# Warm-up matmuls, the row loads of the first norm, and the place of the second norm's scale in a one-core trunk layer

## The chip, the core and the metric

The kernel runs on one core of one Trainium2 chip. The metric is the device time of one execution in microseconds; the median of three runs is given. One further execution was recorded by the hardware profiler, and all lines of the profile and the trace below come from that one. The engines are named as the profile names them: PE (matrix multiply) and PEld (its weight loads), DVE (vector), ACT (scalar), POOL, and SP, which here only issues DMAs.

## What is computed

One layer of a trunk: 512 tokens of width 1024, one batch, all float32. Three residual steps follow each other: a mixer with four branches, a cross-attention to 256 memory tokens, and a convolutional feed-forward part. Cut to what matters here:

```python
def rms_norm(x, g):
    xf = x.astype(jnp.float32)
    y = xf * lax.rsqrt(jnp.mean(xf * xf, axis=-1, keepdims=True) + EPS)
    return (y * g.astype(jnp.float32)).astype(x.dtype)

def cross_attention(h, mem_n, wq, wkv, wo):
    ...
    q = (h @ wq).reshape(bsz, s, XA_HEADS, XA_HEAD_DIM)
    k, v = jnp.split(mem_n @ wkv, 2, axis=-1)
    ...
    sc = jnp.einsum('bshd,bmhd->bhsm', q, k).astype(jnp.float32) * (XA_HEAD_DIM ** -0.5)
    p = jax.nn.softmax(sc, axis=-1).astype(v.dtype)
    ...

    h = rms_norm(x, g[0])                       # first norm
    y = hybrid_mixer(h, w_in[l], ...)
    x = x + rms_norm(y, g[1])
    h = rms_norm(x, g[2])                       # second norm
    mem_n = rms_norm(mem, g[4])
    y = cross_attention(h, mem_n, xa_wq[l], xa_wkv[l], xa_wo[l])
    x = x + rms_norm(y, g[3])
    h = rms_norm(x, g[5])
    y = conv_ffn(h, ...)
    x = x + rms_norm(y, g[6])
```

## The kernel before

**Layout and arithmetic.** The activation is kept transposed: eight tiles x[k] of 128 features by 512 tokens. Every large product is done in three matmuls on two-part operands (`mm3`, L124): each operand is split into a rounded part (name ending in h or hi) that ACT writes by a cast, and a remainder (l or lo) that DVE writes by a subtraction; then hi·hi, hi·lo and lo·hi are added up in PSUM. Weights come in units of 512 KB: SP issues the load (L74), ACT casts (L75), DVE subtracts (L76), and PE uses the unit. The tiles raw, whi and wlo have four buffers each, so the cast of one unit waits until PE has done with the unit four before it.

**The first loop** (L242 to L271) runs over k = 0 to 7. For each k it loads x[k] (256 KB) and the rows of the v, a_lr and sgu-v weights (264 KB; for k = 0 in two pieces of 136 and 128 KB). ACT writes xgh, which is x[k] times the first norm's gain (L253), and casts the weights (L259, L267); DVE writes the remainders; PE then does 12 matmuls of 272 columns into four banks (va, L239) and 6 of 256 columns into two banks (sv, L239). The gains come by a small DMA of 32 bytes a partition on ACT's queue (gn0, L232). The per-token factor of the first norm is not in xg: it is applied later, as a per-partition scale, when the banks are read.

**The factor of the first norm** comes from a second copy of x, laid out in rows of tokens: `RowNorm` (L198) loads eight tiles of 128 tokens by 512 features (row, L207, 256 KB each, 2 MB in all) and ACT squares each with a running sum (L208). `step(n)` does n of them; `rstd()` does all that are still to do, and then the square root on ACT and the reciprocal on DVE (L194, L195). In the loop the eight steps are spread over k = 2 to 7 (L271). After the loop, `bcast_tok` (L216) spreads the factor over the partitions by matmuls with the identity (bctok), and rb0s keeps a copy.

**Order of work.** The program is written in one stream, and a scheduler places the instructions on each engine's queue by its own estimate of when they can run. What is written inside `with tc.high_priority():` goes ahead of all other work that its inputs allow it to pass. That covers `rs0 = xnorm.rstd()` and `rb0 = bcast_tok(rs0)` at L272 to L274. On the chip every engine then takes its queue in order, and DMAs issued by SP go through one queue.

**The second norm** (`residual1`, L701 to L727) runs on DVE and ACT while PE computes keys and values of the memory (L730 to L750). It adds the mixer's output to x, sums the squares into s2, turns s2 into a factor per token by four small matmuls (`rstd_tok`, L181, sumtok), spreads that by four more (bctok), and then writes h2 = x·gain·factor in eight DVE instructions (L725), each followed by a cast and a subtraction (`split`, L150). `wq` (L756) multiplies h2 by the query weights; `scores` (L766) multiplies q by k, takes the maximum over the memory tokens (L779, L780) and the exponential with the scale 1/16 (L783).

Of the kernel before, what the change touches and what calls it, by code (L numbers as in the profile page):

```python
# [16 lines left out]
P = 128  # L17
# [6 lines left out]
EPS = 1e-6  # L24

NSLOT = 76
LOOK = 2
POOL_OUT = (0, 2, 3, 5)

# [10 lines left out]
def tile_trunk(ctx: ExitStack, tc: tile.TileContext, a: dict, out: bass.AP):  # L40
# [13 lines left out]
    def get(name, dt=F32):  # L54
        i = free.pop(0)
        serial[0] += 1
        t = sp.tile([P, S], dt, tag=f"s{i}", name=f"{name}_{serial[0]}")
        held[id(t)] = (i, t)
        return t
# [105 lines left out]
    def gcol(n, k):  # L165
        return pc("norm", n * KT + k)

    ident = cp.tile([P, P], F32, name="ident")
    make_identity(nc, ident)
    ones = cp.tile([P, 1], F32, name="ones")  # L170
# [57 lines left out]
    VA = 256 + 16  # L228
    vps = [bank("B", f"va{t}") for t in range(4)]
    sps = [bank("A", f"sv{t}") for t in range(2)]  # L230
    gn0 = cp.tile([P, KT], F32, name="gn0")
    scalar.dma_start(gn0, a["par"][:, 0:KT])  # L232
    xg, svw = [], []
    xnorm = RowNorm(a["x_rows"], 4, "rs0")

# [4 lines left out]
                              start=k == 0 and i == 0, stop=k == KT - 1 and i == 2)  # L240

    for k in range(KT):  # L242
        sync.dma_start(x[k], a["xT"][k])
        raw = wp.tile([P, 1024], F32, tag="raw", bufs=4, name=f"rawv{k}")
        if k == 0:
            sync.dma_start(raw[:, 0:VA], a["w_vs"][k][:, 0:VA])
            sync.dma_start(raw[:, VA:VA + 256], a["w_vs"][k][:, VA:VA + 256])
        else:
            sync.dma_start(raw[:, 0:VA + 256], a["w_vs"][k])
        if k == 4:  # L250
            sync.dma_start(par, a["par"])
        hi, lo = get("xgh", F32R), get("xgl", F32R)
        scalar.activation(hi, x[k], AF.Copy, scale=gn0[:, k:k + 1])  # L253
        wh = wp.tile([P, 1024], F32R, tag="whi", bufs=4, name=f"whv{k}")
        wl = wp.tile([P, 1024], F32R, tag="wlo", bufs=4, name=f"wlv{k}")
        if k == 0:
            vector.tensor_copy(wh[:, 0:VA], raw[:, 0:VA])
        else:
            scalar.copy(wh[:, 0:VA], raw[:, 0:VA])  # L259
        vector.scalar_tensor_tensor(lo, x[k], gn0[:, k:k + 1], hi.bitcast(F32), op0=ALU.mult, op1=ALU.subtract)  # L260
        vector.tensor_tensor(wl[:, 0:VA], raw[:, 0:VA], wh[:, 0:VA].bitcast(F32), op=ALU.subtract)
        xg.append((hi, lo))
        if k % 2 == 0:
            svw.append((get("svwh", F32R), get("svwl", F32R)))
        c = slice((k % 2) * 256, (k % 2 + 1) * 256)
        sh, sl = svw[-1][0][:, c], svw[-1][1][:, c]
        scalar.copy(sh, raw[:, VA:VA + 256])  # L267
        vector.tensor_tensor(sl, raw[:, VA:VA + 256], sh.bitcast(F32), op=ALU.subtract)
        rows(vps, k, (wh[:, 0:VA], wl[:, 0:VA]), range(4))
        rows(sps, k, (sh, sl), (0, 1))  # L270
        xnorm.step((0, 0, 1, 1, 1, 1, 2, 2)[k])  # L271
    with tc.high_priority():  # L272
        rs0 = xnorm.rstd()
        rb0 = bcast_tok(rs0)  # L274
# [426 lines left out]
    def residual1():  # L701
        with tc.high_priority():
            rs = rstd_tok([ssum[0]], "rs1")
            rb = bcast_tok(rs)
        put(ssum[0])
        s2 = []
        for k in range(KT):
            vector.tensor_tensor(yg[k], rb, yg[k], op=ALU.mult)
            vector.tensor_add(x[k], x[k], yg[k])
            put(yg[k])  # L710
            sq = get("sq")
            scalar.activation(sq, x[k], AF.Square)
            if k == 0:
                s2.append(sq)
            else:
                vector.tensor_add(s2[0], s2[0], sq)
                put(sq)
        with tc.high_priority():
            rs = rstd_tok(s2, "rs2")
            rb = bcast_tok(rs)  # L720
        put(*s2)
        h2 = []
        for k in range(KT):
            hk = get("h2")
            vector.scalar_tensor_tensor(hk, x[k], gcol(2, k), rb, op0=ALU.mult, op1=ALU.mult)  # L725
            h2.append(split(hk, "h2", True))
        return h2  # L727


    kk = [(get("kh", F32R), get("kl", F32R)) for _ in range(4)]  # L730
# [8 lines left out]
    for cb in range(2):  # L739
# [8 lines left out]
                        k == 0, k == KT - 1)  # L748
        for t in range(2):
            vv[t][cb] = split(ps[t], "v")  # L750
    h2 = residual1()
    for t in mem:
        put(*t)

# [11 lines left out]
    def scores(hd, q):  # L766
        pr = [get("p"), get("p")]
        for t2 in range(2):
            ps = bank("C", "sc")
            for i in range(2):  # L770
                t = 2 * t2 + i
                tt = slice(t * P, (t + 1) * P)
                for d in range(2):
                    c = slice(d * 256, (d + 1) * 256)
                    mm3(ps[:, i * 256:(i + 1) * 256], (q[d][0][:, tt], q[d][1][:, tt]),
                        (kk[hd][0][:, c], kk[hd][1][:, c]), d == 0, d == 1)
            serial[0] += 1
            mx = tp.tile([P, 4], F32, tag="mx", bufs=4, name=f"mx_{serial[0]}")
            vector.reduce_max(mx[:, 0:2], ps.rearrange("p (t m) -> p t m", t=2), axis=AX.X)  # L779
            vector.tensor_scalar(mx[:, 0:2], mx[:, 0:2], -1.0 / 16.0, None, op0=ALU.mult)  # L780
            for i in range(2):
                c = slice(i * 256, (i + 1) * 256)
                scalar.activation(pr[t2][:, c], ps[:, c], AF.Exp, bias=mx[:, i:i + 1], scale=1.0 / 16.0,  # L783
                                  accum_out=mx[:, 2 + i:3 + i])
            vector.reciprocal(mx[:, 2:4], mx[:, 2:4])
            for i in range(2):
                c = slice(i * 256, (i + 1) * 256)
                vector.tensor_scalar(pr[t2][:, c], pr[t2][:, c], mx[:, 2 + i:3 + i], None, op0=ALU.mult)
        for d in range(2):
            put(*q[d])  # L790
        return pr
# [198 lines left out]
def _layout(inp):  # L990
    import numpy as np
    i = {k: np.asarray(v) for k, v in inp.items()}

    def mt(w, width=P):
        k, m = w.shape
        return np.ascontiguousarray(
            w.reshape(k // P, P, m // width, width).transpose(2, 1, 0, 3).reshape(m // width, P, (k // P) * width))

    def cols(v):
        v = v.reshape(-1, v.shape[-1])  # L1000
        return v.reshape(v.shape[0], -1, P).transpose(2, 0, 1).reshape(P, -1)

    d = {}
    d["xT"] = np.ascontiguousarray(i["x"][0].T).reshape(KT, P, S)
    d["memT"] = np.ascontiguousarray(
        i["mem"][0].T.reshape(4, 2, P, NMEM).transpose(0, 2, 1, 3)).reshape(4, P, 2 * NMEM)
    w = i["w_in"][0]
    names = ("ab", "ac", "ax", "q", "k", "v", "r", "alr", "su", "sv", "rx", "rg")
    widths = (256,) * 7 + (16,) + (256,) * 4
    seg, o = {}, 0  # L1010
    for n, wd in zip(names, widths):
        seg[n] = w[:, o:o + wd]
        o += wd
    d["w_in"] = mt(np.concatenate([seg[n] for n in ("k", "q", "rx", "su", "rg", "ac", "ax", "ab", "r")], axis=1))
    d["x_rows"] = i["x"][0].reshape(4, P, D)
    d["mem_rows"] = i["mem"][0].reshape(2, P, D)

    def moving(w):
        k, m = w.shape
        return np.ascontiguousarray(  # L1020
            w.reshape(k // 256, 2, P, m // S, S).transpose(3, 0, 2, 1, 4).reshape(-1, P, 2 * S))

    d["w_vs"] = np.concatenate([seg["v"], seg["alr"], seg["sv"]], axis=1).reshape(KT, P, 528)
    d["par"] = np.ascontiguousarray(np.concatenate([
        cols(i["norm_g"][0]), cols(i["sc_conv_w"][0]), cols(i["gla_b_alpha"]), cols(i["gla_norm_g"]),
        cols(i["lru_conv_w"][0]), cols(i["lru_conv_b"]), cols(i["lru_b_a"]), cols(i["lru_b_x"]),
        cols(i["b_gate"][0]), cols(i["ffn_conv_w"][0]), cols(i["ffn_conv_b"])], axis=1))
    d["lam"] = np.ascontiguousarray(cols(i["lru_lambda"]))
    d["ln_g"] = i["sgu_ln_g"][0]
    d["ln_b"] = i["sgu_ln_b"][0]  # L1030
    d["sgu_wT"] = np.ascontiguousarray(i["sgu_w"][0].transpose(2, 0, 1)).reshape(P, S)
    d["sgu_b"] = i["sgu_b"][0]
    d["lru_w_a"] = i["lru_w_a"][0]
    d["lru_w_x"] = i["lru_w_x"][0]
    d["w_alpha"] = i["gla_w_alpha"][0]
    d["w_gate"] = mt(i["w_gate"][0])
    d["w_br"] = np.ascontiguousarray(
        i["w_branch"][0].reshape(4, 2, P, 2, 4, P).transpose(0, 3, 2, 4, 1, 5)).reshape(8, P, 1024)
    d["w_mix"] = mt(i["w_mix_out"][0])
    d["w_q"] = mt(i["xa_wq"][0])  # L1040
    d["w_k"] = mt(i["xa_wkv"][0][:, :D])
    d["w_v"] = moving(i["xa_wkv"][0][:, D:])
    d["w_o"] = mt(i["xa_wo"][0])
    d["w_up"] = mt(i["ffn_w_up"][0])
    d["w_down"] = mt(i["ffn_w_down"][0])
    return {k: np.ascontiguousarray(v) for k, v in d.items()}
# [20 lines left out]
```

## Time and profile before

| | us |
|---|---|
| median of three runs (lowest, highest) | 960.14 (959.26, 961.12) |
| time of the profiled execution | 960.77 |
| its span, from the first to the last instruction | 958.2 |
| busy PE | 943.9 |
| busy PEld | 800.5 |
| busy DVE | 575.0 |
| busy ACT | 420.7 |
| moved by DMA | 98.27 MB |

The span leaves out 2.57 us of the profiled execution's time. PE is busy for all but 14.3 us of the span; the rows that show where it waits are quoted in the prediction. The mean granted clock of PE is 0.997.

### The profile page before, as it was taken

The page shows a single profiled execution, that of the slowest core. Times are in us where ns is not written, and L with a number is a line of the kernel's source. Part 1 is how long each engine was busy: PE and PEld are TensorE (multiplying, and loading weights), DVE is VectorE, ACT ScalarE, POOL GpSimd, SP SyncE. Part 2 cuts the span into 40 slices and gives each one's busy share as a digit, 9 for nine tenths or more (in the row PEclk, how much of TensorE's full clock was granted, in tenths as well). Part 3 has the DMA queues.
Part 4 walks back from the last instruction along what each step waited for, and adds up shares of the span by engine and source line. Part 5 has one row for each costly group of instructions (what it writes and reads, how often), then busy time and mean ns, then how long its engine had stood idle before and what let it go on. Part 6 is the DMA issues. An engine that isn't in the chain of part 4 may idle for free.

```text
span 958.2 us, 12139 instructions
## 1 busy us (share of the span) xinstructions
PE 943.9 (99%) x4782; PEld 800.5 (84%) x4782; DVE 575.0 (60%) x886; ACT 420.7 (44%) x637; POOL 11.9 (1%) x33
## 2 busy tenths in 40 slices
PE   7999999999999999999999999999999999999996
PEld 7888888888888888898888899888888888888885
DVE  5877557445454667359854736887677776622404
ACT  7845336332323534455543645554444444332311
POOL 2000000000000000000000000000000000000001
PEclk9999999999999999999999999999999999999998
DMA  9432231322243422335412420232322323233302
GB/s 334 136 123 89 67 102 52 109 89 92 84 135 129 132 89 80 118 122 187 134 65 66 148 73 2 90 108 88 109 89 97 102 89 102 79 105 99 100 1 88
DMA packets 32648, 98.27 MB, mean 103 GB/s; under 512 B 4288, under 2 KB 7248, under 8 KB 32592
## 3 DMA queue, kind: packets, MB, share of 16 engines
q1 hardware_dynamic: 32416, 97.48, 31.5%
q8 instruction: 37, 0.61, 0.3%
q14 instruction: 19, 0.16, 0.1%
q0 software_dynamic: 32, 0.02, 0.0%
q10 hardware_dynamic: 144, 0.00, 0.0%
HBM read 95.39 MB, written 2.10 MB: 102 GB/s over the span
## 4 chain that ended last, share of the span: by engine, by line
PE 97%; issue 1%; ACT 1%; DVE 0%; DMA 0%; SPq 0%; DVEq 0%
PE up L127 8%; PE up L126 8%; PE up L125 8%; PE gate L125 6%; PE gate L126 6%; PE gate L127 6%; PE dn L125 4%; PE dn L127 4%; PE dn L126 4%; PE win L125 4%; PE win L127 3%; PE win L126 3%; PE wo L125 2%; PE wo L127 2%; PE wo L126 2%; PE br L125 2%
## 5 line engine op out<-in xcount | busy, mean ns | idle before, releaser
L75 ACT CAST whi<-raw 128x1024 fp32r<-128x1024 f32 x158 | 164.4, 1042 | 299.4 <-issue 137.8
L76 DVE TENSOR_TENSOR wlo<-raw,whi 128x1024 fp32r<-128x1024 f32 x158 | 191.2, 1213 | 130.4 <-ACT whi L75 128.8
L127 PE MATMUL up<-h3h,wlo 128*128 128x512 f32 (+1 forms) x368 | 138.2, 376 | 0.0
L126 PE MATMUL up<-h3l,whi 128*128 128x512 f32 (+1 forms) x368 | 138.1, 375 | 0.0
L125 PE MATMUL up<-h3h,whi 128*128 128x512 f32 (+1 forms) x368 | 138.1, 375 | 0.0
L125 PE MATMUL gate<-xgh,whi 128*128 128x512 f32 x256 | 99.9, 390 | 0.0
L127 PE MATMUL gate<-xgh,wlo 128*128 128x512 f32 x256 | 99.7, 389 | 0.0
L126 PE MATMUL gate<-xgl,whi 128*128 128x512 f32 x256 | 99.6, 389 | 0.0
L125 PEld LDWEIGHTS up<-h3h,whi 128*128 128x128 f32 x368 | 69.3, 188 | 12.6
L126 PEld LDWEIGHTS up<-h3l,whi 128*128 128x128 f32 x368 | 69.3, 188 | 12.4
L127 PEld LDWEIGHTS up<-h3h,wlo 128*128 128x128 f32 x368 | 69.3, 188 | 12.4
L352 DVE TENSOR_TENSOR sg<-gate,rb0s 128x512 f32<-128x512 f32 x32 | 22.1, 692 | 80.1 <-PE gate L127 80.1
L546 DVE SCALAR_TENSOR_TENSOR c<-u,par,c 128x511 f32<-128x511 f32 (+1 forms) x88 | 65.0, 746 | 1.3
L125 PE MATMUL dn<-gh,whi 128*128 128x512 f32 x154 | 59.9, 389 | 0.0
L126 PE MATMUL dn<-gl,whi 128*128 128x512 f32 x154 | 59.9, 389 | 0.0
L127 PE MATMUL dn<-gh,wlo 128*128 128x512 f32 x154 | 59.9, 389 | 0.0
L125 PE MATMUL win<-xgh,whi 128*128 128x512 f32 x144 | 57.2, 397 | 0.0
L125 PEld LDWEIGHTS gate<-xgh,whi 128*128 128x128 f32 x256 | 48.1, 188 | 10.0
L126 PEld LDWEIGHTS gate<-xgl,whi 128*128 128x128 f32 x256 | 48.1, 188 | 9.9
L127 PEld LDWEIGHTS gate<-xgh,wlo 128*128 128x128 f32 x256 | 48.1, 188 | 9.9
L127 PE MATMUL win<-xgh,wlo 128*128 128x512 f32 x144 | 56.3, 391 | 0.0
L126 PE MATMUL win<-xgl,whi 128*128 128x512 f32 x144 | 56.1, 390 | 0.0
(348 smaller groups left out, 1728.5 us busy)
## 6 DMA issues: line engine op xcount, KB each, us to landing
raw<-in_w_up SPq DMA_DIRECT2D x44, 512.0 KB, 3.5
raw<-in_w_gate SPq DMA_DIRECT2D x32, 512.0 KB, 3.5
raw<-in_w_in SPq DMA_DIRECT2D x18, 512.0 KB, 4.0
raw<-in_w_down SPq DMA_DIRECT2D x16, 512.0 KB, 3.6
raw<-in_w_br SPq DMA_DIRECT2D x8, 512.0 KB, 3.5
raw<-in_w_mix SPq DMA_DIRECT2D x8, 512.0 KB, 3.5
raw<-in_w_k SPq DMA_DIRECT2D x8, 512.0 KB, 3.5
raw<-in_w_v SPq DMA_DIRECT2D x8, 512.0 KB, 3.5
```

The source lines that it names most:

```text
L75: scalar.copy(hi[:, :n], raw[:, :n])
L76: vector.tensor_tensor(lo[:, :n], raw[:, :n], hi[:, :n].bitcast(F32), op=ALU.subtract)
L125: tensor.matmul(ps, lhsT=w[0], rhs=x[0], start=first, stop=False)
L126: tensor.matmul(ps, lhsT=w[0], rhs=x[1], start=False, stop=False)
L127: tensor.matmul(ps, lhsT=w[1], rhs=x[0], start=False, stop=last)
L352: vector.tensor_tensor(t, ps, rb0s, op=ALU.mult)
L546: vector.scalar_tensor_tensor(dst[:, s:S], src[:, 0:S - s], pc(wname, (taps - 1 - s) * stride + off), dst[:, s:S], op0=ALU.mult, op1=ALU.add)
```

## The change

Three things are edited. First, a tile of ones is filled by DVE and six matmuls of 512 columns on it go to a bank that nothing reads. Second, the loop's row steps are taken out, so that all eight stand in `rstd()` behind the loop; the gains of the first norm and the first piece of the weights come in one DMA on ACT's queue (143 KB), and x[0] is loaded and scaled in two pieces of 256 tokens. Third, h2 is no longer multiplied by the second norm's factor: it is x·gain alone, split as it is made, and the factor (over 16) goes into the maximum and into the scale of the scores' exponential, token by token.

```diff
+    idle = bank("C", "idle")
+    spin = get("spin", F32R)
+    vector.memset(spin.bitcast(F32), 1.0)
+    for _ in range(SPIN):          # SPIN = 6
+        tensor.matmul(idle, lhsT=spin[:, 0:P], rhs=spin, start=True, stop=True)
+    put(spin)
...
-    gn0 = cp.tile([P, KT], F32, name="gn0")
-    scalar.dma_start(gn0, a["par"][:, 0:KT])
+    wg0 = cp.tile([P, VA + KT], F32, name="wg0")
+    gn0 = wg0[:, VA:VA + KT]
+    scalar.dma_start(wg0, a["w_vg"])
...
     for k in range(KT):
-        sync.dma_start(x[k], a["xT"][k])
+        cuts = (slice(0, 256), slice(256, S)) if k == 0 else (slice(0, S),)
+        for c in cuts:
+            sync.dma_start(x[k][:, c], a["xT"][k][:, c])
+        rv = wg0 if k == 0 else raw
...
-        scalar.activation(hi, x[k], AF.Copy, scale=gn0[:, k:k + 1])
+        for c in cuts:
+            scalar.activation(hi[:, c], x[k][:, c], AF.Copy, scale=gn0[:, k:k + 1])
...
-        xnorm.step((0, 0, 1, 1, 1, 1, 2, 2)[k])
     with tc.high_priority():
         rs0 = xnorm.rstd()
...
-        s2 = []
+        s2, h2 = [], []
         for k in range(KT):
...
+            hi, lo = get("h2h", F32R), get("h2l", F32R)
+            scalar.activation(hi, x[k], AF.Copy, scale=gcol(2, k))
+            vector.scalar_tensor_tensor(lo, x[k], gcol(2, k), hi.bitcast(F32), op0=ALU.mult, op1=ALU.subtract)
+            h2.append((hi, lo))
-        with tc.high_priority():
-            rs = rstd_tok(s2, "rs2")
-            rb = bcast_tok(rs)
+        rs = rstd_tok(s2, "rs2")
         put(*s2)
-        h2 = []
-        for k in range(KT):
-            hk = get("h2")
-            vector.scalar_tensor_tensor(hk, x[k], gcol(2, k), rb, op0=ALU.mult, op1=ALU.mult)
-            h2.append(split(hk, "h2", True))
-        return h2
+        qs = cp.tile([P, 8], F32, name="qs")
+        vector.tensor_scalar(qs[:, 0:4], rs[:, 0:4], 1.0 / 16.0, None, op0=ALU.mult)
+        vector.tensor_scalar(qs[:, 4:8], rs[:, 0:4], -1.0 / 16.0, None, op0=ALU.mult)
+        return h2, qs
...
-            vector.tensor_scalar(mx[:, 0:2], mx[:, 0:2], -1.0 / 16.0, None, op0=ALU.mult)
+            vector.tensor_mul(mx[:, 0:2], mx[:, 0:2], qs[:, 4 + 2 * t2:6 + 2 * t2])
...
-                scalar.activation(pr[t2][:, c], ps[:, c], AF.Exp, bias=mx[:, i:i + 1], scale=1.0 / 16.0,
+                scalar.activation(pr[t2][:, c], ps[:, c], AF.Exp, bias=mx[:, i:i + 1],
+                                  scale=qs[:, 2 * t2 + i:2 * t2 + i + 1],
```

**What moves on SP's queue.** The first DMAs of the program, before; in_xT is the transposed x, in_w_vs the weights of the loop, in_x_rows the copy of x in rows:

```order
L243 DMA x_1_86<-in_xT 128x512
L246 DMA rawv_104<-in_w_vs 128x272
L247 DMA rawv_104<-in_w_vs 128x256
L243 DMA x_2_87<-in_xT 128x512
L249 DMA rawv_138<-in_w_vs 128x528
L243 DMA x_3_88<-in_xT 128x512
L249 DMA rawv_169<-in_w_vs 128x528
L207 DMA row_201<-in_x_rows 128x512
L243 DMA x_4_89<-in_xT 128x512
```

The first DMAs of the changed program on the same queue (six equal rows between the first and the last of the row loads are left out):

```order
L215 DMA row_371<-in_x_rows 128x512
...
L215 DMA row_392<-in_x_rows 128x512
L255 DMA x_3_95<-in_xT 128x256 x2
L258 DMA rawv_112<-in_w_vs 128x256
L255 DMA x_4_96<-in_xT 128x512
L260 DMA rawv_147<-in_w_vs 128x528
```

All eight row loads now stand first, ahead of x[0]; the text has them behind the loop, but they lie inside the high-priority block and wait for nothing, so the scheduler set them at the front. Before, the first of them was the eighth DMA and the last the twenty-sixth.

**What moves on ACT.** The start of ACT's queue before (rs_parts are the running sums of the row squares):

```order
L232 DMA gn_100<-in_par 128x8
L175 ACT_TABLE_LOAD
L175 ACTIVATE warm<-ones 128x1
L253 ACTIVATE xgh_107<-x_1_86,gn_100 128x512
L267 CAST svwh_115<-rawv_104 128x256
L253 ACTIVATE xgh_140<-x_2_87,gn_100 128x512
```

And in the changed program (again six equal rows left out):

```order
L241 DMA wg_109<-in_w_vg 128x280
L183 ACT_TABLE_LOAD
L183 ACTIVATE warm<-ones 128x1
L216 ACTIVATE row_371,rs_parts<-row_371 128x512
...
L216 ACTIVATE row_392,rs_parts<-row_392 128x512
L265 ACTIVATE xgh_116<-x_3_95,wg_109 128x256
L202 ACTIVATE rs_49_396<-rs_parts,epsc 128x4
L265 ACTIVATE xgh_116<-x_3_95,wg_109 128x256
```

The eight squares stand ahead of the first xgh, on which the first matmul of the loop waits, and the square root of the first norm stands between the two halves of that xgh.

**What moves on PE.** At the start there were only the loop's matmuls in order; in the changed program it begins:

```order
L173 MATMUL idle_71<-spin_72 128x512 x6
L248 MATMUL va_11_103<-whv_120,xgh_116 128x272
L229 MATMUL bctok_399<-ident,rs_49_396 128x128 x4
L248 MATMUL va_12_104<-whv_120,xgh_116 128x272
L248 MATMUL va_13_105<-whv_120,xgh_116 128x272
```

The broadcast of the first norm's factor came after the loop's last matmul before, and comes after its first now. Before, two of the four small transposes alT stood a third of the way into the products of sv for the tokens 256 to 511 and two at their end; now all four stand directly behind the loop.

The other place on PE is the end of the values of the memory (v) and the start of the queries (q). Before, the sum and the broadcast of the second norm stood inside v:

```order
L126 MATMUL v_3648<-wlo_3606,memh_2984 128x512
L187 MATMUL sumtok_3782<-ones,sq_3745 128x1 x4
L127 MATMUL v_3648<-whi_3605,meml_2985 128x512
...
L125 MATMUL v_3648<-whi_3623,memh_2990 128x512
L221 MATMUL bctok_3790<-ident,rs_443_3787 128x128 x4
L126 MATMUL v_3648<-wlo_3624,memh_2990 128x512
```

In the changed program, with one broadcast gone:

```order
L127 MATMUL v_3659<-wlo_3680,memh_3012 128x512
L128 MATMUL v_3659<-whi_3679,meml_3013 128x512
L195 MATMUL sumtok_3824<-ones,sq_3755 128x1 x4
L126 MATMUL q_3835<-h2h_3757,whi_3697 128x512
L127 MATMUL q_3835<-h2l_3758,whi_3697 128x512
```

The sum now stands behind the last matmul of v and directly ahead of the first of q.

More of the change, by code (lines that the diff above doesn't have):

```diff
@@ L26 @@
 NSLOT = 76
+SPIN = 6
 LOOK = 2
@@ L242, in tile_trunk @@
     for k in range(KT):
-        sync.dma_start(x[k], a["xT"][k])
         raw = wp.tile([P, 1024], F32, tag="raw", bufs=4, name=f"rawv{k}")
+        cuts = (slice(0, 256), slice(256, S)) if k == 0 else (slice(0, S),)
+        for c in cuts:
+            sync.dma_start(x[k][:, c], a["xT"][k][:, c])
+        rv = wg0 if k == 0 else raw
         if k == 0:
-            sync.dma_start(raw[:, 0:VA], a["w_vs"][k][:, 0:VA])
             sync.dma_start(raw[:, VA:VA + 256], a["w_vs"][k][:, VA:VA + 256])
@@ L256, in tile_trunk @@
         if k == 0:
-            vector.tensor_copy(wh[:, 0:VA], raw[:, 0:VA])
+            vector.tensor_copy(wh[:, 0:VA], rv[:, 0:VA])
         else:
@@ L260, in tile_trunk @@
         vector.scalar_tensor_tensor(lo, x[k], gn0[:, k:k + 1], hi.bitcast(F32), op0=ALU.mult, op1=ALU.subtract)
-        vector.tensor_tensor(wl[:, 0:VA], raw[:, 0:VA], wh[:, 0:VA].bitcast(F32), op=ALU.subtract)
+        vector.tensor_tensor(wl[:, 0:VA], rv[:, 0:VA], wh[:, 0:VA].bitcast(F32), op=ALU.subtract)
         xg.append((hi, lo))
@@ L750, in tile_trunk @@
             vv[t][cb] = split(ps[t], "v")
-    h2 = residual1()
+    h2, qs = residual1()
     for t in mem:
@@ L1023, in _layout @@
     d["w_vs"] = np.concatenate([seg["v"], seg["alr"], seg["sv"]], axis=1).reshape(KT, P, 528)
+    d["w_vg"] = np.concatenate([d["w_vs"][0][:, 0:272], cols(i["norm_g"][0])[:, 0:KT]], axis=1)
     d["par"] = np.ascontiguousarray(np.concatenate([
```

## The prediction

> **What bounds the kernel now.** I read the first lines of the page for the engines' shares, then PE's waits, then the chain of waits over the start, because the page leaves almost nothing else to win.
>
> ```profile
> span 958.2 us, 12139 instructions
> PE 943.9 (99%) x4782; PEld 800.5 (84%) x4782; DVE 575.0 (60%) x886; ACT 420.7 (44%) x637; POOL 11.9 (1%) x33
> ```
> ```profile
> PE va L239 <- ACT xgh L253: 4.4, 1, 4.4
> PE sv L239 <- ACT svwh L267: 0.7, 1, 0.7
> PE rb L970 <- DVE rs L967: 0.6, 1, 0.6
> PE sumtok L960 <- ACT sq L943: 0.5, 1, 0.5
> ```
>
> PE is busy 943.9 of 958.2 us, and of its named waits (total, times, longest) the 4.4 us before the first matmul are the only long one. So an edit counts if it moves PE's start, takes matmuls off PE, or makes PE wait; work saved on DVE or ACT counts nothing by itself. The chain (start, length, what) shows the first loop:
>
> ```profile
> 6.90 1.81 PE va L239 x8
> 8.71 1.06 PE sv L239 x5
> 9.78 1.50 PE va L239 x12
> ...
> 24.56 0.71 PE sv L239 x6
> 25.27 0.89 PE bctok L221 x8
> 26.16 2.86 PE sv L239 x24
> 29.02 0.22 PE alT L300 x2
> ...
> 29.95 0.39 PE alT L300 x2
> 30.34 2.15 PE sv L239 x18
> 32.49 0.23 PE win L125
> ```
>
> From 9.78 us each k costs 1.50 + 0.71 = 2.21 us, and seven of them end at 25.27, with no gap. The matmuls of k = 0 are slower: 1.81/8 = 0.226 and 1.06/5 = 0.212 us each, against 1.50/12 = 0.125 and 0.71/6 = 0.118. So k = 0 took from 4.38 to 9.78, 5.4 us for 2.2 us of work. The column PEclk doesn't show this step (it is 1.00 in the windows below); the pace of the matmuls does.
>
> **Part 1: the rows of x.** The order shows the eight row loads first on SP's queue, and the eight squares ahead of the first xgh on ACT. The first matmul then waits for 2 MB that it doesn't use. When do they land? The windows (the last column is GB/s):
>
> ```profile
> 0.00:2.00 2.00, 0.00 (x0) 0.00 (x0) 0.00 (x0) 0.77 (x1) 1.31 (x12) 1.00 0.09 7
> 2.00:4.00 2.00, 0.00 (x0) 0.00 (x0) 0.10 (x1) 1.11 (x3) 1.39 (x5) 1.00 0.84 212
> 4.00:6.00 2.00, 1.27 (x4) 0.95 (x4) 1.30 (x3) 0.47 (x2) 0.00 (x0) 1.00 0.85 272
> 6.00:8.00 2.00, 1.68 (x7) 1.69 (x8) 1.15 (x3) 1.75 (x5) 0.00 (x0) 1.00 1.06 361
> 8.00:10.00 2.00, 2.00 (x13) 2.00 (x12) 2.00 (x6) 1.49 (x4) 0.00 (x0) 1.00 1.00 363
> 10.00:12.00 2.00, 2.00 (x19) 2.00 (x18) 0.87 (x3) 2.00 (x6) 1.36 (x4) 1.00 1.05 403
> ```
>
> By 8 us, 2 x (7 + 212 + 272 + 361) = 1,704 kB had moved. Eight rows and the 143 kB of gains and weights are 2,240 kB: moved by 8 + 536/363 = 9.5 us. Landing comes later:
>
> ```profile
> 3.61 0.72 ACT L253 ACTIVATE xgh<-x,gn 128x512 fp32r<-128x512 f32 x1 [0.88 <-DMA x<-in_xT]
> ...
> 4.12 0.43 SPq L207 DMA_DIRECT2D row<-in_x_rows x1
> ...
> 9.73 0.63 ACT L208 ACTIVATE row<-row 128x512 f32<-128x512 f32 x1 [0.51 <-DMA row<-in_x_rows]
> ```
>
> Row 0 lay behind x[0] to x[2] and their weights, some 1,860 kB with itself, moved by 8.4 us, and its square started at 9.73: 1.3 us of lag. That puts the last row at 10.8 us. On the other side, only 212 and 272 GB/s went in the first windows, beside the gains' 32-byte pieces that the change drops; at 361 throughout from 2 us the 2,240 kB are moved by 8.2 and landed by 9.5. I take 10.0, nearer the fast end because rows of 2 KB replace small pieces. ACT keeps up:
>
> ```profile
> 18.27 0.63 ACT L208 ACTIVATE row<-row 128x512 f32<-128x512 f32 x1
> ...
> 18.91 0.63 ACT L208 ACTIVATE row<-row 128x512 f32<-128x512 f32 x1
> ...
> 23.24 0.17 DVE L213 TENSOR_TENSOR rs_parts<-rs_parts 128x4 f32<-128x4 f32 x1 [1.45 <-ACT row L208]
> 23.50 0.30 ACT L194 ACTIVATE rs<-rs_parts,epsc 128x4 f32<-128x4 f32 x1 [0.29 <-DVE rs_parts L213]
> 23.83 0.18 DVE L195 RECIPROCAL rs<-rs 128x4 f32<-128x4 f32 x1 [0.42 <-ACT rs L194]
> 25.19 0.47 ACT L285 ACTIVATE svt<-sv,rs 128x256 f32<-128x256 f32 x1 [1.39 <-PE sv L239]
> ```
>
> A square every 0.64 us, from 3.6 on, would be done at 8.7, so the loads decide. After the last landing come one square (0.64), the first half of xgh (as the 128x256 scaled copy, 0.47) and about 0.1 of signalling: first matmul at **11.2 us** (10.7 to 12.0), where it was at 4.38.
>
> x[0] itself isn't late: it is next in the queue, 131 kB or 0.35 us behind, under the last square. The weights of k = 1 to 7 land faster than PE uses them (530 kB at 363 GB/s and more is 1.5 us against 2.21).
>
> **Part 2: the ones.** Six matmuls of 512 columns at the slow pace, 0.226 x 512/272 = 0.43 us each, take 2.6 us and end near 4.5 us even if the fill takes as long as a slow vector operation; nothing waits for them. What they could bring is a fast k = 0. But PE then idles about 7 us until 11.2. Both ends: k = 0 runs at the fast pace, or slow throughout. Behind the first va stands bctok, which waits for the square root (0.30) behind that half xgh and the reciprocal (0.18): about 0.55 us after the first matmul. Fast: 0.55 + 0.89 + 17 matmuls (1.50 + 0.71 - 0.125 = 2.1) = 3.5 us. Slow: 0.55 + 2 x 0.89 + 11 x 0.226 + 6 x 0.212 = 6.1 us. No row here shows PE idle for microseconds and then busy again except the start itself, where the pace changed 5.4 us after the first matmul; the same would be 5.7. I take **5.6**, near the slow end.
>
> [...]
>
> So k = 1 starts at 11.2 + 5.6 = 16.8 instead of 9.78: **+7.0 us**, and the loop ends at 32.3. Bounds: 10.7 + 3.5 = 14.2 (+4.4) and 12.0 + 6.1 = 18.1 (+8.3).
>
> **Part 3: from the loop's end to the first win.** Before this took 32.49 - 25.27 = 7.22 us: 48 matmuls of sv, the broadcast (0.89) and the transposes. Now the broadcast is inside k = 0. The transposes come first and wait for four altok copies on ACT; sv for the next tokens waits for the copy of its bank behind them:
>
> ```profile
> 28.28 0.46 ACT L287 ACTIVATE altok<-va,rs 128x16 f32<-128x16 f32 x2
> ```
>
> The last va ends 0.7 us ahead of the loop. Four copies (0.92), one vt and one svt (0.47 each) end 1.2 us behind the loop, under which the transposes fit. Then 48 matmuls at 2.86/24 = 0.119: 5.7. Sum 6.9, so **-0.3 us**. The casts of the next weights stand ahead of altok on ACT, but their loads are out by then. If one were late, PE would wait up to a cast more.
>
> **Part 4: the second norm.** PE loses one broadcast, and one break in v:
>
> ```profile
> 452.74 0.91 PE sumtok L187 x8
> ...
> 455.63 0.89 PE bctok L221 x8
> ```
>
> 0.89, and about 0.1 for the longer matmul after a break: **-1.0 us**. DVE loses eight h and eight h2l and gains eight h2l with scale, but PE didn't wait for it here. The new danger is sumtok, now the last thing ahead of q: it waits for the sum of squares, and all of q is queued behind it.
>
> ```profile
> 451.81 0.68 DVE L716 TENSOR_TENSOR sq<-sq,sq 128x512 f32<-128x512 f32 x1
> ...
> 455.48 1.04 ACT L75 CAST whi<-raw 128x1024 fp32r<-128x1024 f32 x1 [1.52 <-PE v L127]
> ...
> 461.42 1.28 DVE L153 TENSOR_TENSOR h2l<-h,h2h 128x512 fp32r<-128x512 f32 x2
> ```
> ```profile
> 464.34 0.39 PE L125 MATMUL q<-h2h,whi 128*128 128x512 f32 x1
> ```
>
> In old time, v would end at 464.34 - 0.91 - 0.89 = 462.5. The last sum, at 451.81 before, now stands behind two more casts, which wait for PE to release weight buffers, and behind most of eight h2l (0.64 each). I work it out at about 461.7: in time, by less than 1 us. Cost 0, bounds 0 to 2.
>
> The two qs instructions, the multiply in place of a scalar multiply on 128x2, and a scale by address in the exponential lie on DVE and ACT, many microseconds ahead of their use, or beside PE's work: 0.
>
> **The sum.** +7.0 - 0.3 - 1.0 = **+5.7 us**. On the span: 958.2 + 5.7 = 963.9; the profiled execution took 960.77, 2.57 more than its span and 0.63 more than the median. On the median: 960.14 + 5.7 = **965.8 us**.
>
> **The rivals.**
> - *Early start.* The rows land at 9.5 or before and the ones keep PE's pace: k = 1 near 14.0, +4.2 - 1.3, so about 963. For it: DMA ran at 403 GB/s later. Against: the gap of 7 us. Chance 0.12.
> - *A late sum.* The last square is held up by the casts and PE waits 1 to 2 us ahead of q: 967 to 968. For it: a margin under 1 us. Chance 0.14.
> - *Within the noise of before*, because the rows land as early as 9 us, k = 0 is all fast and nothing else waits: 961 to 962. Chance 0.05. About 0.2%, or 1.9 us, is what a measurement of this kernel can tell from no change.
> - *Faster.* The rows cost nothing, because their loads run beside x[0] rather than ahead of it: first matmul near 4.0, k = 0 in 3.5 us at the fast pace, k = 1 at 7.5, -2.3 - 1.3: 956.5. It decides for faster once k = 1 starts before 9.2, the first matmul before 5.7, so 2,240 kB landed by about 4.5 us: some 900 GB/s from 2 us, against 403. This would also be the outcome if the change did what its words say, the rows behind the tiles; the order says it doesn't. Chance 0.02.
>
> **How the numbers follow.** Forecast 0.67, its own range 964 to 967.3. The range for 8 in 10 takes in most of the early start and of the late sum: 962.8 to 968.2. Faster by over 0.2% is the last rival, 0.02; within 0.2% 0.05; slower the rest, 0.93.
>
> **What would show it.** In the changed profile: PE's longest wait is va on xgh, ending at 10.7 to 12; ACT has eight squares ahead of the first xgh, the later ones waiting for row loads; va and sv of k = 0 run at 0.2 us or more each; k = 1 starts near 16.8 and each later k takes 2.21; alT waits for altok by under 0.5 us; no bctok between 440 and 470; sumtok ahead of q without a wait. It is wrong if the first matmul of the loop comes before 9 us, if k = 0 is fast, or if PE has a new wait of over 1 us after the loop.

## The result and the profile after

The changed kernel takes 965.42 us (median of six runs, 964.35 to 967.28) against 960.39 us for the kernel before beside it (959.26 to 961.20). The ratio is 1.0054, with a 95% interval of 1.0041 to 1.0067: slower by 5.0 us. The span of the profiled execution grew from 958.2 to 963.7 us.

PE's waits in the changed kernel (total, times, longest, in us) are again nearly all at the start:

```profile
PE va L248 <- ACT xgh L265: 6.8, 1, 6.8
PE idle L173 <- DVE spin L171: 1.5, 1, 1.5
PE rb L982 <- DVE rs L979: 0.6, 1, 0.6
PE sumtok L972 <- ACT sq L955: 0.5, 1, 0.5
```

The chain of waits over the start (start, length, what) shows what stands ahead of the first matmul of the loop:

```profile
2.21 5.23 DMA row<-in_x_rows
7.45 0.02 issue
7.47 3.31 ACT row L216 x10
10.78 0.41 ACT xgh L265
11.18 0.04 issue
11.23 0.59 PE va L248
11.82 1.95 PE bctok L229 x8
13.77 2.49 PE va L248 x11
16.26 0.86 PE sv L248 x6
17.12 1.51 PE va L248 x12
...
30.41 1.14 PE va L248 x9
31.54 0.02 issue
31.57 0.77 ACT altok L298 x4
32.34 0.36 ACT vt L301
32.70 0.37 ACT svt L296
33.07 0.04 issue
33.12 6.01 PE sv L248 x48
39.13 0.23 PE win L126
```

A row load and the squares lie on the path, then the half xgh, then a slow k = 0 (2.49/11 = 0.226 us a va). The chain shows the last five squares as one stretch, but the loads set their pace: by the trace each of them starts within 0.05 us of the landing of its own load. The last row load was issued at 4.13 us and landed 5.9 us later, at 10.03; its square started at 10.05. k = 1 starts at 17.12 where it started at 9.78; the chain reaches the first win at 39.13 where it was 32.49. After that nothing more is lost. At the second norm 1.2 us come back, by the timeline of PE around the first q:

```profile
468.71 0.39 PE L128 MATMUL v<-whi,meml 128*128 128x512 f32 x1
468.94 0.95 PE L195 MATMUL sumtok<-ones,sq 128*128 128x1 f32 x8
469.75 0.49 PE L126 MATMUL q<-h2h,whi 128*128 128x512 f32 x1
```

sumtok starts 0.23 us behind the last v, the distance at which the v follow each other here. The first q is 5.4 us later than before (464.34), while the first win was 6.6 later.

### The profile page after: what moved, and what is told of

Read it like the earlier page. It is cut to its first block, busy times and chain, and to the rows that moved or that the text cites. A ratio compares the mean times of both kernels' runs of the same rounds, so it can differ in the third digit from the quotient of the medians.

```text
span 963.7 us, 12140 instructions
## 1 busy us (share of the span) xinstructions
PE 946.1 (98%) x4780; PEld 801.9 (83%) x4780; DVE 570.4 (59%) x881; ACT 422.1 (44%) x638; POOL 11.3 (1%) x33
## 4 chain that ended last, share of the span: by engine, by line
PE 96%; issue 1%; ACT 1%; DMA 1%; DVE 0%; SPq 0%; DVEq 0%
PE up L128 8%; PE up L126 8%; PE up L127 8%; PE gate L126 6%; PE gate L128 6%; PE gate L127 6%; PE dn L128 4%; PE dn L127 4%; PE dn L126 4%; PE win L126 4%; PE win L127 3%; PE win L128 3%; PE wo L128 2%; PE wo L126 2%; PE wo L127 2%; PE br L126 2%
```

## The experiments

Every time is given with the ratio to the kernel before, which ran beside it on the same chip. The first four kernels ran against a before of 960.56 us, the next four against 960.09, the last three once each against 960.30.

**Rows in the loop.** The row steps go back to their old place; all else of the change stays.

```diff
         rows(sps, k, (sh, sl), (0, 1))
+        xnorm.step((0, 0, 1, 1, 1, 1, 2, 2)[k])
```

> The change with the row steps put back into the loop, everything else kept. If the row loads and squares at the front are what costs: the first va starts when the six ones end, near 4.5 us; the pace of PE steps up near 6.7, 5 us after the ones began, so k = 1 starts near 7.9 (9.78 before, 17.12 in the change), and with 1.1 us less around the second norm the time is about 957.3, 3 us below before. If another part of the start costs (the merged gains and weights, x[0] in two pieces, the ones): the time stays within 1 us of the change, about 965.

Measured: 958.94 us, ratio 0.9979 (0.9970 to 0.9988): 6 us below the change and 1.6 below the kernel before. The chain in k = 0:

```profile
6.19 0.50 PE sv L248 x2
6.69 1.00 PE va L248 x8
7.70 0.47 PE sv L248 x4
8.16 1.76 PE va L248 x12
```

The va run at the full pace from 6.69 on (1.00/8 = 0.125 each), and k = 1 started at 8.16. The step in PE's pace lies earlier still: the two sv at 6.19 took 0.50 us, against 0.80 in a run where they are slow (see the repeats), and by the start times of the single matmuls it came near 5.2 us, 3.7 us after the ones began (the four va from 4.46 on took 1.07 us, the first four of the kernel before 1.27). The rows at the front were the whole loss: with them back, no cost of the merged DMA, the split x[0] or the ones shows. The expected 957.3 was too low: it counted on an early step, which this profiled execution had and, by their spans, most runs did not (see the repeats).

**No ones.** The fill and the six matmuls are taken out of the change.

```diff
-    spin = get("spin", F32R)
-    vector.memset(spin.bitcast(F32), 1.0)
-    for _ in range(SPIN):
-        tensor.matmul(idle, lhsT=spin[:, 0:P], rhs=spin, start=True, stop=True)
```

> The change without the fill and the six matmuls on ones. If the idle stretch behind them undoes what they do: k = 0 runs at the same slow pace, k = 1 starts at 17.1 within 0.5, and the time is that of the change within 1 us, about 965.4. If the ones still help k = 0: k = 1 starts later, up to 1 us, and the time is 966 to 966.5.

Measured: 965.93 us, 1.0054 (1.0041 to 1.0066), the same ratio as the change. In its profile k = 1 starts at 18.15, but the first va came 1.1 us later too:

```profile
11.85 0.41 ACT xgh L259
12.25 0.04 issue
12.30 0.59 PE va L242
12.89 1.95 PE bctok L223 x8
14.84 2.49 PE va L242 x11
17.33 0.82 PE sv L242 x6
18.15 1.51 PE va L242 x12
```

From the first va to k = 1 it takes 5.85 us, with the ones 5.89, and the parts are equal to 0.04 us. The ones bring k = 0 nothing where they stand. The later start is that of the landing loads (the last row landed at 11.10 in place of 10.03); it wasn't the 17.1 that both theories had counted on. This profiled execution was the slowest of its five.

**Only the second norm.** The kernel before with the edit of `residual1` and `scores` alone (the last two pieces of the diff above).

> The kernel before with the edit of the second norm alone. If the edit is worth the broadcast taken from PE and a break in v: q starts near 463.2 (464.34 before), the time is 1.0 to 1.2 us below before, about 959.3. If sumtok waits for the sum of squares here (the casts on ACT in its way): a wait of 0.5 to 2 us ahead of q and a time equal to before or above it.

Measured: 959.27 us, 0.9987 (0.9978 to 0.9995), 1.3 us below. In the profile the chain reaches the first win at 33.25 (before 32.49): the first va came 0.17 us later, and the step in PE's pace came inside k = 1, whose twelve va took 2.09 us in place of 1.50. The first q starts at 463.90 (464.34): so 1.2 us are gained between. PE waits nowhere from 400 to 560 us. The rival fell: sumtok doesn't wait.

**24 ones** in the change, in place of six (`SPIN = 24`).

> The change with 24 matmuls on ones in place of 6, so that PE is busy until shortly before the first va. If the pace of k = 0 is set by how long PE was busy just before: the ones speed up near 6.7 us and end near 9.5, k = 0 takes 3.5 us in place of 5.9, k = 1 starts near 14.7, and the time is 2.4 us below the change, about 963. If the slow pace of k = 0 comes from its operands (loads still landing, casts not ready): k = 0 still takes 5.9 us and the time is that of the change.

Measured: 964.99 us, 1.0037 (1.0024 to 1.0051). The ones ran from 1.52 to 9.81, 24 in 8.29 us, so they did speed up on the way: 24 at the 0.43 estimated in the prediction would be 10.3, and the shortest took 387 ns, where the six of the change took 628 and more. But here the first va came late, at 12.69, and 2.9 us of idle PE lay between. The chain:

```profile
12.69 0.52 PE va L248 x2
13.21 1.47 PE bctok L229 x8
14.68 2.27 PE va L248 x10
```

k = 0 took 5.14 us, 0.75 less than with six, and most of its va ran at 2.27/10 = 0.227. By the start times of the single matmuls the first two va and half of the broadcast still ran at the full pace; the pace fell near 13.9 us, 4 us after the last of the ones and 1.2 us into the new work. Neither theory was met; the gap had to be closed to tell. The profiled execution was again the slowest of its five (966.49 us, the fastest 963.23), so a gap of 2.9 us needn't be the usual one.

**34 ones**, to close the gap (`SPIN = 34`).

> The change with 34 matmuls on ones, which end near 12 us, so that PE has no or less than 1 us of idle time ahead of the first va. 24 ones left 2.9 us idle and k = 0 took 5.1 us in place of 5.9. If an idle stretch ahead of k = 0 is what slows it: k = 0 now takes about 3.5 us, its va 0.125 each. If k = 0 is slow for another reason: its va still take 0.22 each and k = 0 5 us or more.

Measured: 964.09 us, 1.0041 (1.0026 to 1.0057), 1.3 us below the change by the medians, though the intervals of the ratios overlap. PE's timeline of k = 0:

```profile
8.72 2.65 PE L173 MATMUL idle<-spin 128*128 128x512 f32 x11
12.33 1.13 PE L229 MATMUL bctok<-ident,rs 128*128 128x128 f32 x8 [0.96 <-DVE rs L203]
13.21 0.75 PE L248 MATMUL va<-whv,xgh 128*128 128x272 f32 x4
13.80 0.66 PE L248 MATMUL va<-whv,xgl 128*128 128x272 f32 x4
14.30 0.66 PE L248 MATMUL va<-wlv,xgh 128*128 128x272 f32 x4
```

Every va now runs at full pace (1.50 for 12 in the chain), the broadcast takes 1.13 in place of 1.95, and k = 1 starts at 15.7. (With 34 ones the scheduler sets the broadcast ahead of all va, with 24 behind the second; in the change it stands behind the first.) The operands were no earlier here, since the last row's square started at 10.66 us, 0.6 later than in the change. So it isn't the operands that make k = 0 slow. Besides the place of the broadcast, what differs is what PE did before: 34 ones and 0.96 us of idle time here, six and 6.78 us in the change. Even so the first matmul of the loop waits for the rows, and the kernel stays slower than before.

**Rows behind.** The steps are written ahead of the high-priority block, so that they do stand behind the loop:

```diff
+    xnorm.step(8)
     with tc.high_priority():
         rs0 = xnorm.rstd()
```

SP's queue then has the eight row loads behind the last of w_vs, ACT the eight squares behind the last cast of the loop.

> The change with the eight row steps written ahead of the high-priority block, so that loads and squares stand behind all tiles of the loop, as the change's words say. If only the place of the rows at the front costs: k = 1 starts near 8.2, the loop ends near 23.9 as with the rows in the loop (23.92), and then the eight squares (0.64 us each on ACT, behind the last casts) make the factor late: PE waits 1 to 2 us behind the loop for the broadcast and for the copies that free the sv banks, and the time is about 960, 1 to 2 us above the rows in the loop. If squares behind the loop are hidden by the copies and casts: the time is that of the rows in the loop, 958.9.

Measured: 959.13 us, 0.9987 (0.9978 to 0.9996), equal to the rows in the loop within their intervals. Part of the expectation fell: nothing waits behind the loop.

```profile
21.98 0.63 ACT L216 ACTIVATE row<-row 128x512 f32<-128x512 f32 x1
...
22.98 0.30 ACT L202 ACTIVATE rs<-rs_parts,epsc 128x4 f32<-128x4 f32 x1 [0.29 <-DVE rs_parts L221]
23.31 0.18 DVE L203 RECIPROCAL rs<-rs 128x4 f32<-128x4 f32 x1 [0.42 <-ACT rs L202]
...
25.00 1.05 PE L229 MATMUL bctok<-ident,rs 128*128 128x128 f32 x8
```

ACT runs ahead of PE in the loop and does the squares while PE works on the later k; the factor is ready at 23.5, 1.5 us ahead of the broadcast. What the change's words say would have cost nothing that shows here.

**x[0] first.** In the change, the load of x[0] too is put into a high-priority block, so that its pieces and the first xgh stand ahead of all but one row load and square.

```diff
+        with ExitStack() as first:
+            if k == 0:
+                first.enter_context(tc.high_priority())
             for c in cuts:
                 sync.dma_start(x[k][:, c], a["xT"][k][:, c])
```

> The change with the load of x[0] in the high-priority block too: its two pieces and the first xgh stand ahead of all but one row load and square. If the cost is the wait for the first xgh alone: the first va starts when the ones end, near 4.5 us, and the time drops by 5 us or more, to 960 or less. If the cost is the 2 MB ahead of everything in the loop: the 12 va of k = 0 run early, then PE waits until about 11.6 for the second piece of the weights and until 13 or later for k = 1, which starts at 14 to 15 (17.1 in the change) with PE's pace slow again, and the time is 963 to 964.5.

Measured: 965.43 us, 1.0054 (1.0040 to 1.0068): nothing gained. The first va starts at 4.56, but then PE waits 4.0 us for svwh:

```profile
7.99 4.66 ACT row L216 x14
12.65 0.30 ACT svwh L282
12.99 0.80 PE sv L248 x2
13.79 1.89 PE bctok L229 x8
15.68 0.85 PE sv L248 x4
16.53 1.92 PE va L248 x12
```

The wait only moved: the next weights and x[1] lie behind the 2 MB, and ACT's casts behind the squares. It's the mass of row data ahead of the loop that costs, not the order of the first xgh; the first of the squares above starts at 7.99, right behind the landing of its load at 7.96. The gain was smaller than the 1 to 2.5 us expected, since k = 1 came at 16.53.

**Rows in the loop, no ones** (the first and the second edit together).

> The rows in the loop, the rest of the change kept, without the ones. If the ones are worth the earlier step in PE's pace where no gap follows them: the first va comes near 4.0, the pace steps up near 9.4, k = 1 starts near 9.4 in place of 8.16, and the time is 0.8 to 1.3 us above that with the ones (958.94), about 960. If the ones bring nothing: the same time within 0.4 us.

Measured: 959.18 us, 0.9987 (0.9978 to 0.9996), against 0.9979 (0.9970 to 0.9988) with the ones. k = 1 starts at 9.76 in its profile. The medians differ by 0.24 us and the intervals overlap: what six ones are worth, if anything, isn't shown.

**Three repeats**, one run each, of kernels that had run.

> The same kernel as the rows in the loop, a second look. If the moment at which PE's pace steps up differs from one execution to the next, the start of k = 1 differs from 8.16 us by up to 1.5 us here. If the pace is fixed by the program: 8.16 within 0.2.

> The same kernel as the rows behind the tiles, a second look. There k = 1 started at 9.37 us although the ones and the first loads are those of the rows in the loop. If that was the moment of the step in that execution: another start here, between 8.0 and 9.6. If it is the program: 9.37 within 0.2. In both cases no wait behind the loop.

> The changed kernel, a second look. The first va started at 11.23 us in its profile, at 12.30 with no ones and at 12.69 with 24. If the landing of the row loads differs from one execution to the next: a first va between 11 and 13 here, and the time 964 to 967. If the start is fixed by the program: 11.23 within 0.2.

Measured: 959.13, 960.06 and 965.43 us. The rows in the loop, the same program as above, now start k = 1 at 9.61 in place of 8.16:

```profile
6.15 0.80 PE sv L248 x2
6.94 1.81 PE va L248 x8
8.76 0.85 PE sv L248 x4
9.61 1.69 PE va L248 x12
```

All of k = 0 is slow here (1.81/8 = 0.226). By the single matmuls the step came near 9.9 us here and near 5.2 us there, in one and the same program, and k = 1 moved by 1.5 us. The spans of the ten runs of the first experiment lie in two groups, four from 955.4 to 956.1 us and six from 956.9 to 957.2; the profile shown there has 955.7, this one 957.1. The rows behind start it at 9.44 (9.37 the first time), which both theories allowed, so this repeat tells nothing. The change's first va came at 10.87 (11.23), so its start moves by some tenths; the 11 to 13 that I expected was too late.

Four versions take less time than both kernels: the rows in the loop (0.9979), the same without the ones, the rows behind, and the second norm alone (0.9987 each). Their intervals overlap, and what they share is the edit of the second norm, which alone gives 1.3 us. No gain of the edits at the start is shown.

## Why the prediction was right

The forecast was 965.8 us, the measured median 965.42. The forecast added 5.7 us; the spans of the profiled executions differ by 5.5 and the medians by 5.0 (the median of before rose to 960.39 with three more runs). Step by step:

- **The rows at the front.** The loads were to land at 10.0 and the first va to come at 11.2; the last landed at 10.03 and the va came at 11.23, in a second run at 9.68 and 10.87. The path was the one described: row loads, the last square, half xgh. That it came out to 0.03 us is luck: with the same loads at the front, the last landed at 11.10 (no ones) and 11.50 (24 ones) in other profiles, outside the 9.5 to 10.8 that the prediction allowed. From 2 to 6 us the DMAs moved 286 and 329 GB/s, 212 and 272 before; whether small pieces had held them back there, no run tests. Putting the rows back removed the whole loss (0.9979), and putting x[0] ahead of them did not (1.0054). That settles the mechanism: the row data ahead of the loop's own.
- **The ones.** k = 0 was taken at 5.6 us, between 3.5 and 6.1; it took 5.89, with the step in PE's pace 5.2 us after the first va, where 5.4 was assumed. That what the ones bring is lost in the idle time behind them couldn't be seen in the trace of before; the slow end was the author's estimate. The runs show it: an equal k = 0 without the ones (5.85 us), and full pace (12 va in 1.50 us) once 34 of them reached up to 0.96 us ahead of PE's next work. With 24 ones and 2.9 us of idle time behind them most of k = 0 was slow (0.227 us a va). Together these two steps made +7.3 us (k = 1 from 9.78 to 17.12), forecast +7.0.
- **From the loop's end to the first win.** Forecast -0.3. With seven k of 2.21 behind 17.12 the loop ends at 32.6, and 39.13 - 32.6 = 6.5 against 7.22: -0.7. The copies were done 0.5 us behind the loop, not 1.2, and the 48 matmuls took 6.0 us, not 5.7. The transposes alT cost no time of their own: they ran from 32.45 to 33.05, under the wait for the svt copy, which ended at 33.07. (Before, they stood behind 24 and 30 of the 48 matmuls, as the chain in the prediction shows, not a third of the way in and at the end.)
- **The second norm.** Forecast -1.0 from the broadcast and one break. From the first win to the first q it was 5.4 - 6.6 = -1.2 in the change and as much in the edit alone. The danger of a late sum was real but didn't bite. The timeline of DVE has the last sum of squares here:

```profile
467.24 0.68 DVE L727 TENSOR_TENSOR sq<-sq,sq 128x512 f32<-128x512 f32 x1
```

It ended at 467.92 and sumtok started at 468.94, so 1.0 us was left; under 1 was forecast.
- **The rivals.** The early start needed the six ones to carry over, and they didn't (2.49/11 = 0.226 us a va in k = 0). The late sum needs 1 us more of delay. The faster outcome was tied to the rows costing nothing; rows in the loop and rows behind show that it would have come, but at 959 and not at 956.5. There I had counted on a fast k = 0, which came, and only in part, in one profile of four of these two kernels.

The sum of the parts, +7.3 - 0.7 - 1.2 = +5.4, agrees with the spans (963.7 - 958.2 = 5.5).

## What to carry to other kernels

A block with raised priority takes with it everything written in it, loads included; work that was spread out elsewhere and is then left to such a block jumps to the very front if it waits for nothing. So compare the engines' queues of both programs before you believe the place in the text. Look at the idle time between warm-up work on PE and the real work: six ones that ended 6.8 us ahead left k = 0 as slow as none (5.89 and 5.85 us), 34 that ended 1 us ahead gave it the full pace, and no gain in the time over the kernel before is shown for either. When the start waits for loads, first move the loads that aren't needed behind those that are (here 965.42 against 958.94 us).

## What was not expected of the hardware

- The moment at which PE's pace steps up differs between executions of one program: it came near 5.2 and near 9.9 us with the same ones from 1.52 us on, and k = 1 started at 8.16 and at 9.61.
- After 2.9 us of idle PE behind 24 ones that had reached full pace (387 ns the shortest, 389 the q of the same width) most of k = 0 was slow again (0.227 us a va), but not at once: the pace fell near 13.9 us, while PE had been busy again since 12.69.
- The column PEclk read 1.00 in the windows in which the va took 0.226 us each, against 0.125 later, in the changed kernel (to 16 us) as before; there only the duration of the matmuls shows it. With 24 ones the column read 0.95 from 12 to 14 us, where the pace fell.
- The same eight row loads at the front let the first va start at 10.87, 11.23, 12.30 and 12.69 us in four profiles (two of the change, no ones, 24 ones), each time 1.2 us behind the landing of the last row. Whether this comes from the chip of the run or from chance stays open.
